# A planner of the issue order counts five times the queue time for a SyncE DMA that writes a single partition

## Chip, cores and metric

The kernel runs on one core of one Trainium2 chip. The metric is device time in microseconds (us) of one execution; the time before is the median of 3 runs, 1483.42 us (1481.35 to 1484.54).

## What is computed

One layer of a hybrid block on x of shape (1, 2048, 1024), all float32. Two branches read the same normalised input, and their gated outputs meet in one projection:

```
hn   = rmsnorm(h, mix_norm_g)
proj = hn @ w_in        # u_ssm 512 | gate_ssm 512 | q 512 | k 512 | v 512 | gate_attn 512
# SSM: 32 groups of 16 channels, 64 complex states per group, a linear recurrence over 2048 steps
y = Re(C x) + D u
zz = gelu(y) @ w_glu + b_glu
y_ssm = val * sigmoid(gate) * silu(gate_ssm)          # val, gate = halves of zz
# stick-breaking attention: 8 heads of 64, strictly causal, blocks of 128 queries
z = (rmsnorm(q) @ rmsnorm(k).T) * 64 ** -0.5
w = exp(log_sigmoid(z) + sum of log_sigmoid(-z) over the later keys)   # keys before the query only
y_att = (w @ v) * silu(gate_attn)
h = h + concat(y_ssm, y_att) @ w_out
h = h + sigmoid(rmsnorm(h, ple_norm_g) @ w_ple_gate) * (p @ w_ple_proj)
```

The attention weights of one query are a cumulative product over the keys. The kernel uses this: with s(j) the running product of sigmoid(-z), the sum of w * v becomes a sum of s times the differences of neighbouring rows of v.

## The kernel before

**Precision and tiles.** Every matmul runs as three products of float32r pieces (hi*hi, hi*lo, lo*hi), so each operand is split into two tiles, mostly by `split` (L511: a copy on ScalarE, a subtraction on VectorE). `wst` is the stage for a weight tile as it comes from HBM (L486); `w_w` is the pair that ScalarE (L491, L513) and VectorE (L65, L76) make of it.

**Stages.** The start (`phase_u`, to about 116 us) normalises x and computes u. Then the SSM is worked in batches, beside the gate matmuls `ps_sg` and the first projections of the attention (116 to 336 us). A skewed loop of 40 steps follows: the heads go in four pairs, pair hp is 8 steps behind pair hp-1, and each pair has 16 blocks of 128 queries. One step does an attention block for up to two pairs (`attn_block`) and the projections of a block that comes two steps later (`attn_proj`). From step 26 the weights `w_glu` are loaded (`glu_load`, eight tiles of 256 KB), from step 30 the GLU units run (`glu_z`, `glu_unit`), and then come products of weights that the last stage needs. The last stage (1152 us on) multiplies by w_out and w_ple_gate and writes the output.

**One block of attention.** `attn_proj` loads `xt` (L717, 1 MB, from `hn`), multiplies (`ps_q`, L745), copies half of the result to `part` (L751) and adds the halves to `qn` (L65 on VectorE). Then the differences of v: L753 copies 127 rows of v from `qn` to the v tile, shifted by one partition, and L755 copies the last row, alone, to partition 0 of the next block's v tile. GpSimd subtracts (L756), which waits for these DMAs. `rs_qk` (L507, GpSimd) and `qn` (L65) normalise q and k, TensorE turns them (`ps_tq`), ScalarE and VectorE write `q`, `k` (L788) and `g` (L791). `attn_block` computes `ps_z` (L812), ScalarE takes the sigmoid to `px` (L816), GpSimd masks the diagonal part of the block (L819, only its first chunk), VectorE scans (L821), TensorE turns (`ps_wt`, L526), ScalarE copies to `ws` (L835), TensorE multiplies by v (`ps_o`, L843), and `yat` goes to HBM by L847. `ps_tq` and `ps_wt` share one pair of PSUM banks, so a turned `ps_wt` waits until `g` has been read out of the `ps_tq` before it.

**DMA queues.** Nearly all DMAs are issued by SyncE, which the profile calls SP, in one order. An instruction that waits on SP holds back all behind it.

**What sets the order.** The program is written out once, and then `arrange` (L1556) orders each engine anew. `plan` (L1322) gives each instruction its predecessors and a modelled length from `duration` (L1289): a time on its engine, a delay until others see it, and for a DMA its bytes. `list_schedule` (L1448) takes in turn, on the engine that is free first, the ready instruction of the lowest rank; a DMA occupies its issuing engine for its modelled time only, and its data are there after a shared link of 290 KB a us and fixed delays. `best_order` (L1523) does this six times forwards and backwards; the ranks of a turn are the modelled finishing times of the one before. Of the six orders it keeps the one with the smallest modelled end, and `arrange` writes it down as a chain of dependencies on each engine. So one number in `duration` reaches every engine's order, and the instructions themselves stay the same.

Of the kernel before, what the change touches and what calls it, by code (L numbers as in the profile page):

```python
# [1288 lines left out]
def duration(i, name, outs, ins, psum):  # L1289

    n = max([a[1] for a in outs + ins] or [1])
    eng = str(i.engine).split(".")[-1]
    if name == "InstDMACopy":
        return (0.6 if eng == "Pool" else 0.45), 0.0
    if name == "InstMatmult":
        cols, kind = outs[0][1], ins[0][2]
        if i.is_transpose:
            return (0.031 if ins[0][0] <= 64 else 0.109), 0.11
        if "float32r" in kind or "bfloat16" in kind:
            return max(cols / 2400.0 + 0.0136, 0.107) / (2 if ins[0][0] <= 64 else 1), 0.11  # L1300
        half = min(outs[0][0], ins[0][0]) <= 64
        return (0.5 if outs[0][0] <= 32 else 1 if half else 2) * max(cols / 1160.0, 0.056), 0.12
    if eng == "Activation":
        return (0.05 if psum else 0.094) + n * 0.00083, 0.065 if psum else 0.03
    if eng == "Pool":
        if name == "InstTensorTensor" and "pow" in str(i.op).lower():
            return 0.35 + 0.15 * n, 0.08
        base, slope = {"InstMemset": (0.04, 0.0008), "InstTensorCopy": (0.4, 0.001), "InstTensorScalarPtr": (0.25, 0.001), "InstTensorScalarAffineSelect": (0.14, 0.0008)}.get(name, (0.12, 0.00186))
        return base + slope * n, 0.09
    if name == "InstTensorScalarPtr" and i.is_tensor_tensor_scan:  # L1310
        return 0.05 + n * 0.0022, 0.03
    if name in ("InstMemset", "InstTensorCopy", "InstTensorScalarPtr") and not psum and not i_tt(i):
        return 0.07 + n * 0.0006, 0.03
    return 0.07 + n * 0.00104, 0.03


def i_tt(i):

    return getattr(i, "is_scalar_tensor_tensor", False)


def plan(tc, pools):  # L1322
# [28 lines left out]
    for k, i in enumerate(mybir_i):  # L1351
# [65 lines left out]
        pre.append(need)  # L1417
        soft.append(loose - need)
        length.append(duration(i, type(i).__name__, outs, ins, psum) + ((outs[0][0] * outs[0][1] * 4 if type(i).__name__ == "InstDMACopy" else 0), shares(i, type(i).__name__, read, psum)))
        if type(i).__name__ == "InstMatmult":  # L1420
            mode[k] = "rows" if ins[0][0] <= 64 else "cols" if outs[0][0] <= 64 else "all"
# [194 lines left out]
```

## Time and profile before

| | |
|---|---|
| median of 3 runs | 1483.42 us |
| the profiled execution: own time | 1483.66 us |
| its span in the profile | 1481.9 us, at a granted TensorE clock of 0.995 |
| busy share of the span | TensorE (PE) 97%, its weight loads (PEld) 83%, VectorE (DVE) 68%, ScalarE (ACT) 55%, GpSimd (POOL) 32% |
| DMA packets | 178,909, 238.21 MB |

The profile is of one execution. Its own time is 1.76 us more than its span. A row of the timeline gives the start in us, the time from the start of the first to the end of the last instruction of a group, the engine, line, operation and tiles with the count, and in brackets how long the engine was idle before and what ended that idle time. Matmuls are pipelined: one may start before its predecessor's end.

### The profile page before, as it was taken

The page shows a single profiled execution, that of the slowest core. Times are in us where ns is not written, and L with a number is a line of the kernel's source. Part 1 is how long each engine was busy: PE and PEld are TensorE (multiplying, and loading weights), DVE is VectorE, ACT ScalarE, POOL GpSimd, SP SyncE. Part 2 cuts the span into 40 slices and gives each one's busy share as a digit, 9 for nine tenths or more (in the row PEclk, how much of TensorE's full clock was granted, in tenths as well). Part 3 has the DMA queues.
Part 4 walks back from the last instruction along what each step waited for, and adds up shares of the span by engine and source line. Part 5 has one row for each costly group of instructions (what it writes and reads, how often), then busy time and mean ns, then how long its engine had stood idle before and what let it go on. Part 6 is the DMA issues. An engine that isn't in the chain of part 4 may idle for free.

```text
span 1481.9 us, 33584 instructions
## 1 busy us (share of the span) xinstructions
PE 1443.8 (97%) x13068; PEld 1223.0 (83%) x13068; DVE 1011.5 (68%) x1814; ACT 810.8 (55%) x1764; POOL 473.7 (32%) x512
## 2 busy tenths in 40 slices
PE   6999999999999999999999999999999999999998
PEld 5999989988888888887788877887777888777776
DVE  8953877976567876677667775656787557844444
ACT  5654555655556765566555664566655445533332
POOL 3121364422221212121112123544234554433432
PEclk9999999999999999999999999999999999999999
DMA  8886846644433433334333455867477546423221
GB/s 292 283 284 209 246 140 195 198 158 148 142 134 107 154 119 106 117 112 144 113 109 120 130 149 175 235 224 203 118 243 246 184 152 214 140 70 100 87 73 55
DMA packets 178909, 238.21 MB, mean 161 GB/s; under 512 B 65744, under 2 KB 121024, under 8 KB 167616
## 3 DMA queue, kind: packets, MB, share of 16 engines
q1 hardware_dynamic: 176368, 227.49, 47.6%
q0 software_dynamic: 2384, 8.59, 2.0%
q8 instruction: 103, 1.69, 0.5%
q14 instruction: 54, 0.44, 0.1%
HBM read 166.94 MB, written 64.90 MB: 156 GB/s over the span
## 4 chain that ended last, share of the span: by engine, by line
PE 79%; DVE 9%; ACT 3%; issue 3%; DMA 3%; POOL 2%; SPq 0%; POOLq 0%; ACTq 0%; DVEq 0%
PE ps_q L745 21%; PE ps_o L843 7%; PE ps_z L812 6%; PE ps_wt L526 4%; PE ps_g L707 4%; PE ps_h L709 4%; PE ps_h L708 4%; PE ps_h L707 4%; PE ps_g L709 3%; PE ps_g L708 3%; PE ps_u L541 1%; PE ps_u L543 1%; PE ps_u L542 1%; POOL sx L912 1%; PE ps_sg L541 1%
## 5 line engine op out<-in xcount | busy, mean ns | idle before, releaser
L821 DVE TENSOR_TENSOR_SCAN px<-px,ps_z 128x512 f32<-128x512 f32 (+3 forms) x320 | 339.4, 1085 | 101.8 <-ACT px L816 66.1
L745 PE MATMUL ps_q<-w_w,xt 64*128 64x512 f32 x2784 | 375.9, 399 | 0.7 <-ACT part L751 0.5
L745 PEld LDWEIGHTS ps_q<-w_w,xt 64*128 64x128 f32 x2784 | 271.0, 186 | 39.0 <-DVE qn L65 1.3
L835 ACT ACTIVATE ws<-ps_wt 128x512 f32<-128x512 f32 (+3 forms) x320 | 161.1, 538 | 76.9 <-PE ps_wt L526 70.7
L816 ACT ACTIVATE px<-ps_z 128x512 f32<-128x512 f32 (+3 forms) x320 | 159.6, 535 | 75.8 <-PE ps_z L812 73.8
L812 PE MATMUL ps_z<-k,q 64*128 64x512 f32 (+3 forms) x960 | 138.9, 380 | 3.3 <-DVE px L821 2.3
L843 PE MATMUL ps_o<-ws,v 128*64 128x128 f32 x2176 | 135.9, 277 | 0.0
L843 PEld LDWEIGHTS ps_o<-ws,v 128*64 128x64 f32 x2176 | 117.8, 137 | 18.2 <-issue 15.5
L507 POOL TENSOR_TENSOR rs_qk<-rs_qk,mhalf 128x4 f32<-128x4 f32 x64 | 68.0, 1062 | 166.6 <-DVE rs_qk L72 163.8
L526 PEld LDWEIGHTS ps_wt<-ident,px 64*128 64x128 f32 x2176 | 96.0, 138 | 26.0 <-ACT ws L835 6.2
L526 PE MATMUL ps_wt<-ident,px 64*128 64x64 f32 x2176 | 102.2, 224 | 3.1 <-ACT ws L835 2.7
L812 PEld LDWEIGHTS ps_z<-k,q 64*128 64x128 f32 x960 | 88.2, 186 | 20.3 <-issue 4.9
L819 POOL TENSOR_SCALAR_AFFINE_SELECT px<-px 128x128 f32<-128x128 f32 x128 | 40.6, 327 | 170.9 <-ACT px L816 169.7
L756 POOL TENSOR_TENSOR v<-qn,v 128x128 f32<-128x128 f32 x64 | 31.4, 491 | 174.1 <-DMA v<-qn 160.4
L541 PE MATMUL ps_u<-xt,w_w 128*128 128x256 f32 x256 | 75.5, 296 | 8.1 <-ACT w_w L491 6.9
L65 DVE TENSOR_TENSOR yr<-sx,yr 128x512 fp32r<-128x512 f32 x64 | 50.6, 813 | 42.2 <-ACT yr L513 41.5
L543 PE MATMUL ps_u<-xt,w_w 128*128 128x256 f32 x256 | 74.1, 295 | 2.0 <-DVE w_w L76 2.0
L542 PE MATMUL ps_u<-xt,w_w 128*128 128x256 f32 x256 | 74.9, 294 | 0.5 <-DVE xt L65 0.5
L1026 POOL TENSOR_TENSOR sg<-sg,h 128x512 f32<-128x512 f32 x28 | 39.6, 1414 | 95.6 <-DVE sg L65 94.1
L513 ACT ACTIVATE yr<-sx 128x512 fp32r<-128x512 f32 x64 | 39.1, 627 | 55.9 <-POOL sx L912 26.2
L65 DVE TENSOR_TENSOR qn<-ps_q,part 128x512 f32<-128x512 f32 x54 | 36.8, 681 | 38.5 <-ACT part L751 35.4
L513 ACT ACTIVATE yr<-yq 128x512 fp32r<-128x512 f32 x48 | 30.3, 631 | 55.5 <-PE ps_h L709 24.2
(438 smaller groups left out, 3488.0 us busy)
## 6 DMA issues: line engine op xcount, KB each, us to landing
xt<-hn SPq DMA_DIRECT2D x58, 1024.0 KB
hn<-xt SPq DMA_DIRECT2D x16, 1024.0 KB
h<-h SPq DMA_DIRECT2D x64, 256.0 KB
wst<-in_w_in_dram SPq DMA_DIRECT2D x48, 256.0 KB
xg<-hn SPq DMA_DIRECT2D x12, 1024.0 KB
out_dram<-sg SPq DMA_DIRECT2D x32, 256.0 KB
x<-in_x_dram SPq DMA_DIRECT2D x14, 512.0 KB
h<-in_x_dram SPq DMA_DIRECT2D x28, 256.0 KB
```

The costliest lines, as they stand in the source:

```text
L526: e.nc.tensor.transpose(ps[h][:, 64 * k:64 * k + 64], v[r], e.ident[r, r])
L541: mm(out, wh, xh, start=first, stop=False)
L542: mm(out, wh, xl, start=False, stop=False)
L707: mm(out, xh, wh, start=first, stop=False, skip_group_check=more)
L708: mm(out, xh, wl, start=False, stop=False, skip_group_check=more)
L709: mm(out, xl, wh, start=False, stop=last, skip_group_check=more)
L745: nc.tensor.matmul(o, xt[r, a, c], A.w[c][r, b], start=c + s == 0, stop=c == NC8 - 1 and s == 2)
L812: nc.tensor.matmul(z[:, :n], q[half[h], a], A.k[ch][half[h], b, :n], start=s == 0, stop=s == 2)
L816: nc.scalar.activation(px[:, :n], z[:, :n], AF.Sigmoid, scale=-(HD ** -0.5))
L821: nc.vector.tensor_tensor_scan(rv, rv, z[:, :n][:, ::-1], initial=1.0 if carry[h] is None else carry[h], op0=ALU.mult, op1=ALU.bypass)
L835: nc.scalar.activation(dst, ps, AF.Copy, bias=1.0, scale=-1.0)
L843: nc.tensor.matmul(po[half[h], :P], A.v[sb][:, h], w[:, h, b], start=sb == i, stop=sb == 0)
```

## The change

```diff
@@ -1291,6 +1291,8 @@ def duration
     n = max([a[1] for a in outs + ins] or [1])
     eng = str(i.engine).split(".")[-1]
     if name == "InstDMACopy":
+        if eng != "Pool" and outs and outs[0][0] == 1:
+            return 2.2, 0.0
         return (0.6 if eng == "Pool" else 0.45), 0.0
     if name == "InstMatmult":
```

`outs[0][0]` is the number of partitions written. The new case holds for 64 DMAs, all on SP: the 60 copies of a last row at L755 and four copies of one row at L727 (from `vl`, a spare tile, to the v tile). They are the same DMAs as before; only the planner counts 2.2 us of SP's time for each, in place of 0.45 us. Lines behind L1293 have moved by two. No instruction is added or removed.

The order changes in stretches and stays in others. By the times of the profile before it differs at 16 to 35 us, 91 to 106, 116 to 336, 475 to 526, 683 to 755, 816 to 1152 and in one place near 1258; it is the same, up to single neighbours, at 345 to 475, 526 to 683, 755 to 816 and in the rest of the last stage. Three places follow.

**SP, 686 to 705 us: the first loads of `w_glu`.** Two of the eight tiles have been issued at 674 us; the rows below begin with the next ones. Rows with a minus are those of before, rows with a plus those of the change.

```order
-L486 DMA wst<-in_ssm_w_glu_dram 128x1x512 x3
+L486 DMA wst<-in_ssm_w_glu_dram 128x1x512 x2
 L717 DMA xt<-hn_69 128x2048
 L753 DMA v<-qn 127x128
 L755 DMA v<-qn 1x16x8
 L847 DMA ya_103<-yat 128x128
-L486 DMA wst<-in_ssm_w_glu_dram 128x1x512
+L486 DMA wst<-in_ssm_w_glu_dram 128x1x512 x2
 L717 DMA xt<-hn_61 128x2048
```

The fifth tile of `w_glu` has moved behind one block's `xt`, both copies of v, and the store of another block's result.

**ACT at the same place, 689 to 697 us.** `w_w<-wst` at L513 is the first half of the split of such a tile. Before:

```order
L788 ACTIVATE k<-ps_tq,gq 128x128
L513 ACTIVATE w_w<-wst 128x512
L791 ACTIVATE g<-ps_tq 128x128
L816 ACTIVATE px<-ps_z 128x512 x2
L751 ACTIVATE part<-ps_q 128x512
L513 ACTIVATE q<-ps_tq 128x128
L513 ACTIVATE w_w<-wst 128x512
L788 ACTIVATE k<-ps_tq,gq 128x128
```

With the change:

```order
L788 ACTIVATE k<-ps_tq,gq 128x128
L816 ACTIVATE px<-ps_z 128x512
L791 ACTIVATE g<-ps_tq 128x128
L816 ACTIVATE px<-ps_z 128x512
L751 ACTIVATE part<-ps_q 128x512
L513 ACTIVATE q<-ps_tq 128x128
L513 ACTIVATE w_w<-wst 128x512 x2
L788 ACTIVATE k<-ps_tq,gq 128x128
```

The third tile's split stood between one block's `k` and `g`. Now it stands with the fourth tile's behind the next block's `q`, ahead of that block's `k` and `g`.

**DVE, 703 to 709 us**, in the same stretch: `qn` of L76 is the one from which the next two v copies on SP read; the two `px` rows are the scans of a block's diagonal chunk, which come behind GpSimd's L819.

```order
 L65 TENSOR_TENSOR qn<-qn,rs_qk 128x256
+L821 SCALAR_TENSOR_TENSOR px<-px,ps_z 128x384 x2
 L76 SCALAR_TENSOR_TENSOR qn<-ps_q,rs_148,part 128x512
-L821 SCALAR_TENSOR_TENSOR px<-px,ps_z 128x384 x2
-L764 TENSOR_REDUCE ssq<-sq 128x4
```

`qn` has moved behind the two scans.

**ACT, 851 to 857 us: where the GLU stage starts.** `zr<-zt` is the first half of a split of the GLU's input, `ws` is what TensorE's next turning waits for. Before:

```order
L759 ACTIVATE gn<-qn 128x128
L513 ACTIVATE zr<-zt 128x512 x2
L835 ACTIVATE ws<-ps_wt 128x2x2x64
L513 ACTIVATE zr<-zt 128x512
L835 ACTIVATE ws<-ps_wt 128x2x2x64
L816 ACTIVATE px<-ps_z 128x256 x2
```

With the change:

```order
L835 ACTIVATE ws<-ps_wt 128x2x2x64 x2
L816 ACTIVATE px<-ps_z 128x512 x2
L762 ACTIVATE sq<-qn 128x256
L759 ACTIVATE gn<-qn 128x128
L513 ACTIVATE zr<-zt 128x512
L835 ACTIVATE ws<-ps_wt 128x8x64
L513 ACTIVATE zr<-zt 128x512
L835 ACTIVATE ws<-ps_wt 128x8x64
```

Both `ws` of 128x2x2x64 now stand ahead of all pieces of `zr`, and the pieces alternate with the `ws` of the next chunk.

## The prediction

> **What bounds the kernel now.** I read the page first, for the engine that sets the end, then the busy time by stretches, for the idle time that a new order could win, and then the timelines of the places where the order changes.
>
> ```profile
> PE 1443.8 (97%) x13068; PEld 1223.0 (83%) x13068; DVE 1011.5 (68%) x1814; ACT 810.8 (55%) x1764; POOL 473.7 (32%) x512
> PE 79%; DVE 9%; ACT 3%; issue 3%; DMA 3%; POOL 2%; SPq 0%; POOLq 0%; ACTq 0%; DVEq 0%
> ```
>
> TensorE is busy for 1443.8 of 1481.9 us, and the chain that ended last lies on it for 79%. SP's own issues take 0% of the chain. No instruction is added or removed, so TensorE's work stays as it is, and all that an order can win is its idle time: 1481.9 - 1443.8 = 38.1 us, spread over the program. The next view gives the stretches with the new order: the window, its length, then the busy time of PE, PEld, DVE, ACT and POOL.
>
> ```profile
> 116.00:336.00 220.00, 214.19 (x1779) 201.43 (x1778) 169.73 (x298) 118.49 (x275) 83.79 (x60) 1.00 0.61 191
> 683.00:722.00 39.00, 34.80 (x410) 27.52 (x408) 26.33 (x42) 23.01 (x54) 6.62 (x12) 0.97 0.39 111
> 850.00:866.00 16.00, 15.06 (x194) 11.94 (x192) 14.85 (x23) 13.44 (x28) 4.26 (x6) 1.00 0.59 138
> 905.00:1107.00 202.00, 200.08 (x1905) 160.47 (x1902) 140.09 (x183) 122.46 (x244) 86.86 (x88) 1.00 0.66 203
> ```
>
> TensorE is idle for 5.8 us in the first, 4.2 in the second, 0.9 in the third and 1.9 in the last. The second is the densest in idle time, 39 us that hold 4.2; there the new order matters most.
>
> **The charge itself: nothing.** The 64 DMAs remain, so their real time on SP stays.
>
> ```profile
> L755 SPq DMA_DIRECT2D v<-qn x56: 567/2338/6853, 195.9 to 1017.0; - x56
> L727 SPq DMA_DIRECT2D v<-vl x4: 503/544/552, 311.0 to 783.4; - x4
> ```
>
> The columns are least, median and greatest ns. At L755 a median of 2.338 us fits the new 2.2 us. The four of L727 write one partition too and take 0.544 us, so the time is not that of a single partition. The timeline of SP shows whose it is:
>
> ```profile
> 433.39 0.67 SPq L753 DMA_DIRECT2D v<-qn  x1
> 434.14 2.34 SPq L847 DMA_DIRECT2D ya<-yat  x1
> 436.55 0.99 SPq L755 DMA_DIRECT2D v<-qn  x1
> ```
>
> Here a store of 128 partitions came between the two copies of v and paid 2.34 us, and L755 got by with 0.99. So the charge falls on whatever stands directly behind L753, which copies 127 rows. Nearly always that is L755, before and after, so the planner's SP becomes right in sum though the reason is wrong, and I price the charge at 0: SP has no share of the chain, and its slack covers the places where a store takes L755's place. If that cover were gone, one such swap would cost 2.34 - 0.99 = 1.35 us of SP once.
>
> [...]
>
> **683 to 722 us, first stall.** SP, then ACT, then PE:
>
> ```profile
> 686.35 7.89 SPq L486 DMA_DIRECT2D wst<-in_ssm_w_glu_dram  x3
> 694.30 0.47 SPq L717 DMA_DIRECT2D xt<-hn  x1
> 695.74 0.68 SPq L753 DMA_DIRECT2D v<-qn  x1
> 696.47 6.39 SPq L755 DMA_DIRECT2D v<-qn  x1
> ...
> 703.66 0.61 SPq L486 DMA_DIRECT2D wst<-in_ssm_w_glu_dram  x1
> 704.33 0.46 SPq L717 DMA_DIRECT2D xt<-hn  x1
> 705.59 0.64 SPq L753 DMA_DIRECT2D v<-qn  x1
> ```
>
> ```profile
> 692.34 0.63 ACT L513 ACTIVATE w_w<-wst 128x512 fp32r<-128x512 f32 x1 [2.90 <-DMA wst<-in_ssm_w_glu_dram]
> ...
> 694.92 0.63 ACT L513 ACTIVATE w_w<-wst 128x512 fp32r<-128x512 f32 x1 [0.16 <-DMA wst<-in_ssm_w_glu_dram]
> 695.46 0.35 ACT L788 ACTIVATE k<-ps_tq,gq 128x128 fp32r<-128x128 f32 x1
> 695.80 0.42 ACT L762 ACTIVATE sq<-qn 128x256 f32<-128x256 f32 x1
> 696.23 0.28 ACT L791 ACTIVATE g<-ps_tq 128x128 f32<-128x128 f32 x1
> ```
>
> ```profile
> 689.68 1.55 PE L745 MATMUL ps_q<-w_w,xt 64*128 64x512 f32 x12
> 693.18 0.34 PE L526 MATMUL ps_tq<-ident,qn 64*128 64x64 f32 x4 [1.96 <-ACT g L791]
> ```
>
> ACT waits 2.90 us for the third tile of w_glu with `g` behind it, and PE stands idle for 1.96 us because `ps_tq` needs `g`. In the new order `g`, two `px` and `part` pass ahead of that split, so this stall goes. What is late next: both splits now stand ahead of the next block's `k` and `g`, and the fourth tile lands only at 694.92. Before, `k`, `sq` and `g` came behind that split and `g` ended at 696.23 + 0.28 = 696.51; now it is `k`, one `px` and `g`, about 0.1 longer. TensorE's next `ps_wt` needs that `g`, so it starts at 696.6, as before, whatever TensorE does sooner ahead of it. The stall moves by 3 us of program and comes back: **+0.1 us**, between -1.96 (TensorE gets work to cover it) and +1 (the fourth tile slips).
>
> **The two stalls behind it.** GpSimd waits for the v copies, and all of it behind L756 waits too, the masks of L819 among them, on which DVE's scans and then PE's next `ps_z` wait:
>
> ```profile
> 706.22 0.46 POOL L756 TENSOR_TENSOR v<-qn,v 128x128 f32<-128x128 f32 x1 [4.26 <-DMA v<-qn]
> ...
> 716.27 0.45 POOL L756 TENSOR_TENSOR v<-qn,v 128x128 f32<-128x128 f32 x1 [5.84 <-DMA v<-qn]
> ```
>
> ```profile
> 707.39 0.39 PE L812 MATMUL ps_z<-k,q 64*128 64x512 f32 x1
> 707.97 0.96 PE L812 MATMUL ps_z<-k,q 64*128 64x512 f32 x5 [0.18 <-DVE px L821]
> ...
> 716.18 0.39 PE L812 MATMUL ps_z<-k,q 64*128 64x512 f32 x1
> 718.28 0.97 PE L812 MATMUL ps_z<-k,q 64*128 64x512 f32 x5 [1.70 <-DVE px L821]
> ```
>
> Five of these matmuls span 0.96 us and one 0.39, so one follows another after (0.96 - 0.39) / 4 = 0.14 us. The stalls cost 707.97 - 707.39 - 0.14 = 0.44 and 718.28 - 716.18 - 0.14 = 1.96 us.
>
> The first v copy was issued at 695.74 and landed at 706.2, behind 256 KB of w_glu and 1 MB of `xt`. With the change `xt` has not the fifth tile ahead of it and can go when `ps_q` has released its buffer, at 689.68 + 1.55 = 691.2, some 3 us earlier; `part` and `qn` come about 2 us earlier as well. The copy should land by 702, and GpSimd is no longer late: **-0.44 us** (0 to -0.44). The second copy was issued at 705.59 and landed at 716.3, again behind a w_glu tile and an `xt`. The sixth tile can now go once its buffer is free, near 701, since L755 no longer blocks SP until 702.9; that wins up to 2 us for the `xt` behind it. Against this, `qn` now stands behind two scans:
>
> ```profile
> 704.77 0.75 DVE L76 SCALAR_TENSOR_TENSOR qn<-ps_q,rs,part 128x512 f32<-128x512 f32 x1 [0.99 <-ACT part L748]
> 706.96 1.80 DVE L821 TENSOR_TENSOR_SCAN px<-px,ps_z 128x384 f32<-128x384 f32 x2 [1.44 <-POOL px L819]
> ```
>
> If the scans start near 704.5, `qn` ends near 704.5 + 1.8 + 0.75 = 707.05, against 705.5, and the copy is issued 1.5 us later, while its queue is free 2 us earlier. Half of the stall is my middle: **-1.0 us** (0 to -1.96).
>
> **850 to 866 us.**
>
> ```profile
> 851.58 2.21 ACT L513 ACTIVATE zr<-zt 128x512 fp32r<-128x512 f32 x2
> 853.67 0.39 ACT L835 ACTIVATE ws<-ps_wt 128x256 f32<-128x256 f32 x1
> 853.93 1.20 ACT L513 ACTIVATE zr<-zt 128x512 fp32r<-128x512 f32 x1
> 854.97 0.44 ACT L835 ACTIVATE ws<-ps_wt 128x256 f32<-128x256 f32 x1
> ```
>
> ```profile
> 853.12 1.55 PE L745 MATMUL ps_q<-w_w,xt 64*128 64x512 f32 x12
> 855.46 0.71 PE L526 MATMUL ps_wt<-ident,px 64*128 64x64 f32 x16 [0.79 <-ACT ws L835]
> ```
>
> Three pieces of `zr`, 3.4 us, stood ahead of or between the two `ws`, and PE was idle for 0.79 us. Both `ws` now stand ahead of them: **-0.8 us**. The pieces go between later `ws`, one of 1.20 us ahead of each, so the stall may come back there: 0 is the other end.
>
> **The other stretches.** At the start, 16 to 35 us, TensorE waits for a chain over GpSimd, ACT and DVE that has the same members in a slightly different order; I take 0. In 116 to 336 and 905 to 1107 us the reshuffle is wide, and I cannot follow each wait by hand. TensorE's idle time there, 5.8 and 1.9 us, bounds the gain at 7.7; a loss of as much is my estimate of the other end. I take 0 as the middle.
>
> **The sum**: 0 + 0.1 - 0.44 - 1.0 - 0.8 = -2.1 us. Against the profiled execution's 1483.66 this gives 1481.6; that execution is 0.24 us above the median of the runs, 1483.42. I predict **1481.6 us**.
>
> **Rivals.**
> *Stalls only change place (1483.5 us).* For it: the stall at 693 already comes back at 696.6 by the sum above, and TensorE at 97% leaves a new order little. The wrong address of the charge belongs here, too: the planner gets SP's sum right by accident, and SP decides nothing. Against it: the wait for v at 706 and 716 hangs on two queue entries that really move.
> *Slower, the chain v, GpSimd, scan, qn, next v (1488 us).* In the new order of DVE the `qn` from which the second copy reads stands behind two scans, which wait for L819, which waits behind L756 for the first copy. If that copy still lands at 706, the scans end at 706.96 + 1.80 = 708.8, `qn` at 709.5, and the second copy starts at 709.6 in place of 705.59: 4.0 us later, and the stall of 1.96 becomes 6. That is 1483.66 + 4.0 = 1487.7. It decides from a landing of the first copy later than about 704. For it: the copy is issued behind 1 MB of `xt` in the same queue, and L755 took 6.39 us there. Against it: the fifth tile, which delayed `xt`, is out of its way.
> *Faster, the wide stretches win too (1477 us).* If half of their 7.7 us of idle time goes as well, 1481.6 - 3.9 = 1477.7. Nothing in the rows says that it does; the idle time only allows it.
>
> **How the numbers follow.** I give the forecast 0.40, the stalls in new places 0.25, the slower chain, or a new wait of its size in the wide stretches, 0.22, and the wide gain 0.13. The range reaches from 1474 (1483.66, less the 7.7 us of the wide stretches and the 2.1 of the sum) to 1490 (1483.66, plus 4.0 for the chain and 2.4, the size of the two v stalls, once more elsewhere). A measurement of this kernel can tell about 0.2%, 3.0 us, from no change, which puts the bounds at 1480.5 and 1486.4. The forecast lies 1.1 us inside the lower one: of its 0.40 I put 0.17 below, 0.19 within and 0.04 above. With the other cases: faster 0.30 (0.17 + 0.13), same 0.40 (0.19 + 0.21 of the second), slower 0.30 (0.04 + 0.04 + 0.22).
>
> **What would show it.** Right: PE's idle time between 683 and 722 us falls from 4.2 to about 3, the row of L756 near 706 has no wait for the DMA worth 4 us, the first `ps_wt` behind 695 us is released by `g`, and the `ps_wt` near 855 has no wait for `ws`. L755's median stays near 2.3 us and L727's near 0.54. Wrong: `qn` of L76 later than 708 with a longer idle time behind it (the slower chain), or PE's idle time in 116 to 336 or 905 to 1107 us off by more than 2 us, where my sum has 0.

## The result and the profile after

The change made the kernel slower: 1498.69 us (median of 4 runs, 1495.13 to 1500.25) against 1482.68 us before on the same chips (1481.35 to 1484.54), a ratio of 1.0104 with a 95% interval of 1.0092 to 1.0116. The prediction was 1481.6 us, with a range of 1474 to 1490. The page of the profile after, its first part and its chain:

```profile
span 1498.4 us, 33594 instructions
...
PE 1452.3 (97%) x13068; PEld 1228.0 (82%) x13068; DVE 1014.4 (68%) x1814; ACT 812.1 (54%) x1764; POOL 467.5 (31%) x512
...
PE 77%; DVE 8%; DMA 5%; ACT 4%; issue 3%; POOL 3%; SPq 0%; POOLq 0%; DVEq 0%; ACTq 0%
```

The span has grown by 16.5 us, and it falls into two parts. TensorE's idle time went from 38.1 to 46.1 us, +8.0. Its busy time went from 1443.8 to 1452.3 us, +8.5, although it ran the same 13068 records: the same work took longer. To see where, the program is cut at places where both orders stand alike, so that each stretch holds the same matmuls. The columns are the window, its length, PE's busy time with its records, the granted clock, and the DMA share and GB/s. Before:

```profile
0.00:106.10 106.10, 90.63 (x800) 0.95 0.84 295
106.10:364.40 258.30, 252.49 (x2204) 1.00 0.59 186
673.60:756.90 83.30, 79.10 (x1002) 0.98 0.38 117
807.10:1143.90 336.80, 333.95 (x3202) 1.00 0.64 191
```

After:

```profile
0.00:108.60 108.60, 92.48 (x801) 0.94 0.82 287
108.60:379.50 270.90, 258.68 (x2204) 0.97 0.56 178
689.20:770.40 81.20, 78.31 (x1004) 0.98 0.36 117
820.50:1160.00 339.50, 334.71 (x3202) 1.00 0.62 189
```

| stretch | change in us | of it idle | predicted |
|---|---|---|---|
| start | +2.5 | +0.7 | 0 |
| SSM batches to the first attention blocks | +12.6 | +6.4 | 0, bounded at 7.7 with the GLU's |
| first w_glu loads | -2.1 | -1.3 | -1.3 |
| GLU stage | +2.7 | +1.9 | -0.8 |

The place that the prediction worked out improved, and the stretch that it took at 0 lost 12.6 us. There the granted clock is 0.97 on the mean, and finer windows, the first two from the end of the start, show why:

```profile
70.20:73.60 3.40, 2.10 (x26) 1.00 0.96 340
73.60:77.10 3.50, 3.50 (x19) 0.51 1.03 376
189.70:193.10 3.40, 1.12 (x7) 1.00 0.25 92
193.10:196.50 3.40, 3.40 (x10) 0.50 0.24 84
322.80:326.20 3.40, 1.11 (x11) 1.00 0.32 116
326.20:329.60 3.40, 3.08 (x14) 0.51 0.63 201
343.30:346.70 3.40, 2.10 (x33) 1.00 0.93 322
346.70:353.50 6.80, 6.03 (x42) 0.50 0.59 226
281.90:285.30 3.40, 2.14 (x19) 1.00 0.01 2
285.30:288.70 3.40, 2.45 (x22) 1.00 0.52 189
```

In four of these pairs a window of 3.4 us in which TensorE was idle for 1.3 to 2.3 us is followed by one or two such windows at half the clock, and each of these, where TensorE works throughout, costs another 1.7 us, half of 3.4 by its clock of 0.50 or 0.51. In the last pair the idle time lies on both sides of a border, 1.3 and 0.9 us, and the clock stays. In matmuls of one kind, step by step behind the stall that ends at 192.41 us:

```profile
192.41 0.47 PE L707 MATMUL ps_qk<-w_w,xg 128*128 128x512 f32 x1 [2.27 <-DVE gsq L65]
192.72 0.39 PE L708 MATMUL ps_qk<-w_w,xg 128*128 128x512 f32 x1
192.95 0.47 PE L709 MATMUL ps_qk<-w_w,xg 128*128 128x512 f32 x1
193.22 0.63 PE L707 MATMUL ps_qk<-w_w,xg 128*128 128x512 f32 x1
193.64 0.63 PE L708 MATMUL ps_qk<-w_w,xg 128*128 128x512 f32 x1
```

The step from one to the next is 0.23 us from 192.72 to 192.95 and 0.42 from 193.22 to 193.64. Both executions have 10.2 us at half the clock near 30 us. Behind that and ahead of the end, before had one such window, the 3.4 us from 719.5, right after the stall at 716 of the prediction:

```profile
716.10:719.50 3.40, 1.70 (x14) 1.00 0.00 0
719.50:722.90 3.40, 3.40 (x27) 0.51 0.39 104
```

After has five stretches of six windows in all (73.6, 193.1, 326.2, 346.7 and 711.9 us; the rows of the last stand with the run warm below). Half of TensorE's busy time in them is (3.50 + 3.40 + 3.08 + 6.03 + 3.00) / 2 = 9.5 us, against 3.40 / 2 = 1.7 us before: 7.8 of the 8.5 us by which the busy time grew.

The three longest stalls of the long stretch, 2.27, 2.21 and 1.68 of its 12.2 us of idle time, are of one kind: TensorE's next instruction needs a PSUM bank that the GELU's chain (`gsq`, ACT and DVE in turn) still reads. The one of 0.93 us ahead of the third waits likewise for a gate's product (`sg`).

```profile
286.25 0.46 PE L461 MATMUL ps_y<-us,tp 128*128 128x128 f32 x2 [2.21 <-DVE gsq L65]
...
324.29 0.55 PE L812 MATMUL ps_z<-k,q 64*128 64x128 f32 x6 [0.93 <-DVE sg L65]
326.52 2.07 PE L745 MATMUL ps_q<-w_w,xg 64*128 64x512 f32 x8 [1.68 <-DVE gsq L65]
```

Before had one stall of this kind there:

```profile
316.35 0.97 PE L745 MATMUL ps_q<-w_w,xg 64*128 64x512 f32 x6 [1.57 <-DVE gsq L65]
```

### The profile page after: what moved, and what is told of

Same layout as the page of the kernel before. It is cut to its first block, busy times and chain, and to the rows that moved or that the text cites. A ratio compares the mean times of both kernels' runs of the same rounds, so it can differ in the third digit from the quotient of the medians.

```text
span 1498.4 us, 33594 instructions
## 1 busy us (share of the span) xinstructions
PE 1452.3 (97%) x13068; PEld 1228.0 (82%) x13068; DVE 1014.4 (68%) x1814; ACT 812.1 (54%) x1764; POOL 467.5 (31%) x512
## 4 chain that ended last, share of the span: by engine, by line
PE 77%; DVE 8%; DMA 5%; ACT 4%; issue 3%; POOL 3%; SPq 0%; POOLq 0%; DVEq 0%; ACTq 0%
PE ps_q L745 21%; PE ps_o L843 7%; PE ps_z L812 6%; PE ps_wt L526 4%; PE ps_g L707 3%; PE ps_h L707 3%; PE ps_h L709 3%; PE ps_h L708 3%; PE ps_g L709 3%; PE ps_g L708 3%; PE ps_u L543 1%; PE ps_u L542 1%; PE ps_u L541 1%; POOL sx L912 1%; DVE rot L65 1%
## 5 line engine op out<-in xcount | busy, mean ns | idle before, releaser
L819 POOL TENSOR_SCALAR_AFFINE_SELECT px<-px 128x128 f32<-128x128 f32 x128 | 41.5, 334 | 175.0 <-ACT px L816 167.1
L513 ACT ACTIVATE yr<-sx 128x512 fp32r<-128x512 f32 x64 | 39.2, 628 | 56.4 <-POOL sx L912 26.1
L513 ACT ACTIVATE yr<-yq 128x512 fp32r<-128x512 f32 x48 | 30.3, 631 | 56.4 <-PE ps_h L709 28.6
```

## The experiments

All times are medians; every ratio is to the kernel before, on the same chip, with its 95% interval. The planner's "own count" in the expectations is the modelled end of an order, replayed with the costs of before: 1411.8 us for the order of before and 1419.9 us for the change's. Replayed with the new charge, the order of before still ends at 1416 to 1417. So by the very costs that the change gave it, the planner found a worse order than the one it had; these are its own numbers, not times. The search has not settled when it stops: from the fifth to the sixth forward pass its order of before went from 1414.0 to 1411.8, and with the charge it went from 1419.9, which was kept, to 1422.9. The diffs below show the deciding lines only, some in short form, with the name of the run as a comment; the code around them is left out.

**Where: one half of each order.** `new` is the change's order, `old` that of before; they are joined where both hold the same instructions on every engine.

```diff
+    order = splice(old, start, new, (400,), True)    # early_new; late_new: False
```

> The order of the change up to about 415 us of the program, the order of before behind it. Theory 'early': the loss sits in the wide stretch ahead of 400 us, where the change's first matmuls behind 400 us came 15.2 us later than before's; then 1483 + 15 = 1498 us (1495 to 1500). Rival 'everywhere': every reordered stretch loses in proportion to its length; the early ones hold about half of the reordered time, then 1490 us (1488 to 1493).

> The order of before up to about 415 us, the order of the change behind it. Theory 'early': 16.5 us of delay at the end less 15.2 us at 400 us leave 1.4, so 1484.5 us (1482 to 1487). Rival 'everywhere': half of the loss, 1490 us (1488 to 1493).

Measured: early_new 1494.74 us, 1.0076 (1.0061 to 1.0091); late_new 1487.14 us, 1.0019 (1.0006 to 1.0031). Of the change's 1.04%, 0.76% go with the order of the first 415 us and 0.19% with the rest. Both times lie just outside the ranges of 'early' (0.3 us below and 0.1 above) and 5 and 3 us off the 1490 of 'everywhere'.

**Why: the charge, or the search.**

```diff
+    for k in single[:1]:      # first1; rest63: single[1:]; l753: the 64 copies of 127 rows
+        length[k] = (2.2,) + tuple(length[k][1:])
```

> The planner counts 2.2 us for the first of the 64 single-partition copies alone (the copy of v's last row near 196 us); the other 63 cost 0.45 us as before. Theory 'search': what the charge says of the queue does not matter; any small nudge near 200 us throws the six turns of the search onto another order, and the time goes with that order: 1490 to 1500 us. Rival 'charge': the loss comes from what the 64 charges do to SP's order, each its share; one of 64 gives 1483.5 us (1482 to 1485).

> The planner counts 2.2 us for all of the 64 single-partition copies but the first. Theory 'search': another order again, no worse than by chance; nearly all of the charge is there, yet the time may lie anywhere between 1480 and 1500 us, and I expect it nearer to before, 1486 us (1482 to 1491), as the order ahead of 200 us stays that of before. Rival 'charge': 63 of 64 shares of the loss, 1498 us (1495 to 1501).

> The planner counts 2.2 us for the 64 copies of 127 partitions (L753), behind which the slow issue stands, and 0.45 us again for the single-partition ones. Theory 'wrong address': the change lost because the charge stood on the wrong DMA; with the right one the order is as good as before or better: 1484 us or less (1478 to 1486). Theory 'search': it is one more nudge, and the order gets worse as the planner's own count of it, replayed with the old costs, gets worse. That count goes with the five times measured so far at about 1.8 us for each us; this order's is 5.2 us above that of before, so 1493 us (1489 to 1497).

Measured: first1 1496.18 us, 1.0085 (1.0070 to 1.0100); rest63 1486.84 us, 1.0027 (1.0015 to 1.0039); l753 1491.86 us, 1.0055 (1.0040 to 1.0070). One charge out of 64, 1.75 us on one instruction near 196 us, costs 12.3 us alone (1496.18 - 1483.84), where all 64 cost 16; the other 63 without it cost 3.0. The loss is not a sum over the DMAs. The profile of first1 has a granted clock of 0.96 from 39.6 to 81.8 us and of 0.98 from 117.7 to 348, where the change's has 0.95 from 39 to 82.5 and 0.98 from 118.5 to 351.2; on TensorE the one charge leads to the change's own order up to about 460 us of the planner's time. So first1 says which charge brought the early order; it is not a second, independent order. Nor does the charge on the DMA of 127 rows help, behind which the slow issue stands; there the time that the theory 'search' worked out from the planner's count came true (1489 to 1497).

Three more kernels nudge the search without saying anything of these DMAs, or say it only once.

```diff
-        return (0.6 if eng == "Pool" else 0.45), 0.0
+        return (0.6 if eng == "Pool" else 0.4411561), 0.0     # sp044
-def best_order(ops, pre, soft, length, mode, rows, turns=6):
+def best_order(ops, pre, soft, length, mode, rows, turns=9):  # turns9
+        # last_only: the charged lengths in the sixth forward pass alone
```

> No charge on a single-partition DMA; the cost of every DMA on SP goes from 0.45 to 0.4411561 us, a change of 2% that says nothing of the queue. Theory 'search': any such nudge lands on another order, and this one's own count, replayed with the old costs, is 2.3 us below that of before; at 1.8 us for each us this gives 1480 us (1476 to 1483.5), faster than both kernels. Rival 'chance': the planner's count says nothing at this distance, and a new order is as a rule worse: 1484 to 1492 us.

> No cost is changed; the search makes nine turns instead of six and keeps the order that its own count likes best, 0.5 us below the one of before. Some 2500 of 11720 matmuls stand elsewhere. Theory 'chance': among orders that the planner counts as equal the chip differs by several us, and a new one is rather worse, as the 2% nudge of all of SP's DMAs was (1488.8): 1487 us (1483 to 1493). Rival 'the planner's count decides': 1483 us (1481.5 to 1484.5).

> All 64 single-partition copies are counted at 2.2 us, but only in the sixth and last forward pass of the search; the five before it and all backward passes count 0.45 us, and the sixth order is kept. Theory 'search': one pass with the new count moves few instructions (some 500 of 11720 matmuls stand elsewhere than before, against some 4400 with the change); the loss needs the ranks to drift over six turns, so 1485.5 us (1482 to 1489). Rival 'charge': the charge itself pushes SP's neighbours to bad places, in one pass as well as in six: 1495 to 1499 us.

Measured: sp044 1488.82 us, 1.0031 (1.0019 to 1.0043); turns9 1484.82 us, 1.0008 (0.9999 to 1.0018); last_only 1486.00 us, 1.0019 (1.0009 to 1.0028). A change of 2% that means nothing costs 5 us, although the planner counts its order as the better one: here my reading of the planner's count failed, and its count is no guide below a few us. turns9 fits 'chance' and misses the other range by 0.3 us. The full charge in the last pass alone costs 2.7 us; the 16 us came only with the charge in every pass. How many passes it takes was not tested.

**What a stall is worth, and whether filling one place helps.**

```diff
+    order = splice(old, start, new, (640, 845), False)                            # place12
+    move(line, gsq_step, sg); move(line, gsq_last, rot); move(line, gsq_sigmoid, swp)  # gsq_back
+            nc.tensor.matmul(pq[0], xt[:, 0, 0], A.w[0][:, 0], start=True, stop=True)  # warm, ten times
```

> The order of before, but from about 665 to 880 us that of the change: the two places on which the prediction's gains rest. Theory 'local gains are real': where the change's own run went through 685 to 755 us, its delay fell from 15.6 to 13.4 us, and by 860 us to 12.3; so about 2 to 3 us faster than before, 1481 us (1479 to 1483). Rival 'stalls only change place': the same as before, 1483.8 us (1482.5 to 1485.5), as the planner's own count says, which differs by 0.1 us.

> The change's order with three instructions put back where before had them: near 188 us, on VectorE the two steps of one gsq chain ahead of the sg and of the rot product, on ScalarE its sigmoid ahead of the two half copies of swp. Theory 'stall and clock': the stall of 2.3 us at 190 us was this chain's, and the 3.4 us at a granted clock of 0.5 behind it were the stall's; both go, 2.3 + 1.7 = 4 us, so 1494.7 us (1493 to 1497) and no low clock near 193 us. Rival 'idle only': the stall goes and the clock falls all the same, 1496.4 us. Rival 'moves on': the next instruction waits in its place, 1498.7 us as the change.

> The change's order, with ten matmuls more that have no use (128x512, into a PSUM bank that the next group overwrites), placed ahead of the six matmuls before TensorE's stall of 2.6 us at 709.6 to 712.4. Theory 'idle brings the low clock': with the stall filled, the 3.4 us at a granted clock of 0.5 that followed it do not come; from 705 to 725 us the kernel gains up to 1.7 us on the change's own course, 1497.5 us (1494 to 1500). Rival 'the low clock has another cause': it comes all the same near 712, and the ten matmuls cost up to 1 us.

Measured: place12 1482.83 us, 0.9994 (0.9986 to 1.0003). Within the interval that is no change, and the value lies in the ranges of both theories. In its trace the local gains are there, and a new stall gives part back:

```profile
697.17 0.59 PE L526 MATMUL ps_wt<-ident,px 64*128 64x64 f32 x12 [2.44 <-ACT g L791]
```

This is the wait for `g` that the prediction saw move from 693 to 697 us, now with 3.4 us at half the clock behind it.

gsq_back: 1503.08 us, 1.0121 (1.0106 to 1.0136), not faster than the change, and above all three expectations. In its trace the stall at 190 us is gone, and by 194 us it had gained 4.1 us, as the first theory had it. Then the next projection waits instead, and the clock falls there:

```profile
198.37 0.50 PE L707 MATMUL ps_qk<-w_w,xg 128*128 128x512 f32 x1 [2.83 <-ACT qn L735]
```

```profile
195.80:199.20 3.40, 0.83 (x4) 1.00 0.03 10
199.20:202.60 3.40, 3.40 (x10) 0.51 0.17 54
```

The third theory, that the stall moves on, fits the trace: to put this one wait right wins nothing. That holds for this wait; the others were not tried.

warm: 1497.33 us, 1.0100 (1.0084 to 1.0115). The change's own windows around its stall at 709.6 to 712.4, and those of warm:

```profile
708.50:711.90 3.40, 1.47 (x10) 1.00 0.80 252
711.90:715.40 3.50, 3.00 (x24) 0.51 0.21 57
```

```profile
708.00:712.00 4.00, 4.00 (x51) 1.00 0.29 90
712.00:716.00 4.00, 4.00 (x56) 1.00 0.25 81
```

With ten useless matmuls in the stall the half clock does not come, and warm gains 1.6 us on the change's course: it is 706.53 - 704.06 = 2.47 us ahead at the `ps_o` in front of the stall and 715.60 - 711.54 = 4.06 at the second `ps_wt` behind it. In one profiled execution each, but with the sign and size expected, idle time brought the low clock, at a cost of up to 1.7 us for each 3.4. The time of the whole program does not show it (1.0100 against 1.0104 for the change, with overlapping intervals): at the end of the two profiles warm is 1498.4 - 1495.2 = 3.2 us ahead, so 0.9 of the 4.06 was lost again behind this place.

**What the charge speaks of.** Is SP's time worth anything, and whose are the 2.3 us?

```diff
+        nc.sync.dma_start(A.v[i + 1][:1]..., vr[P - 1:])                     # twice755, behind L755, unseen by the planner
+        nc.sync.dma_start(e.two_d[16 * A.hp + i:16 * A.hp + i + 1], vr[P - 1:])   # twice_free, likewise
-    nc.sync.dma_start(vb[1:], vr[:P - 1])                                     # split753
+    nc.sync.dma_start(vb[1:113], vr[:112])
+    nc.sync.dma_start(vb[113:], vr[112:P - 1])
```

> The order of before, with a second, identical copy of the last row of v behind each of the 60 copies at L755 (the planner does not see it; 60 DMAs more on SP, of 0.5 to 2.3 us each). Theory 'SP is free': SP has no share in the chain, so the time of these DMAs costs next to nothing, 1484.5 us (1482.5 to 1487). Rival 'SP's time counts': if what the charge speaks of were worth charging, 60 such copies would cost a good part of 60 x 0.57 = 34 us, 1495 us or more.

> The order of before, with a second DMA of the same last row behind each of the 60 copies at L755, into 60 rows of a scratch tensor in HBM that nothing else uses, so that it waits for nothing; the planner does not see it. The run with a second copy into the same place does not settle what SP's time is worth, since each second copy there waited 3 to 4 us for the first to land and held SP. Theory 'SP is free': 60 more issues cost next to nothing, 1484.5 us (1482 to 1487). Rival 'SP's time counts': at 0.5 to 2.3 us each the copies hold up the next xt and v, and a good part of 30 to 130 us appears, 1495 us or more.

> The order of before, with the copy of 127 rows of v (L753) cut in two, 112 rows and 15 rows, one directly behind the other; the planner sees one copy of 127 rows. [...] Rival 'the single partition is the slow one': L755 stays at 2.3 us, one more DMA a block makes it 1484 us or more.

Measured: twice755 1539.54 us, 1.0369 (1.0326 to 1.0412), far from what I expected. Its timeline shows what the extra copy did:

```profile
460.74 3.91 SPq L755 DMA_DIRECT2D v<-qn  x1
468.07 0.50 SPq L757 DMA_DIRECT2D v<-qn  x1
```

It writes where the first one writes, so the program lets it be issued only when that one has landed, 468.07 - 464.65 = 3.4 us later, and all of SP waits. This run prices a wait on SP of that size, at 56 / 60 = 0.9 us a block; it says nothing of SP's issue time. twice_free, with a free destination, does: 1485.00 us, 1.0008 (0.9999 to 1.0017). Its 60 extra issues last 0.42 us at the median and cost no more than 0.17%. Issues of 2.3 us or more were not added in any run.

split753: 1480.01 us, 0.9973 (0.9962 to 0.9984): **faster than both kernels**, and closer together, 1478.4 to 1480.5. The copies of its v rows, 112, 15 and then the single one (L758 here):

```profile
L753 SPq DMA_DIRECT2D v<-qn x64: 517/534/3906, 194.7 to 1036.4; - x64
...
L755 SPq DMA_DIRECT2D v<-qn x64: 818/852/927, 195.3 to 1037.0; - x64
...
L758 SPq DMA_DIRECT2D v<-qn x56: 526/546/1779, 196.3 to 1013.5; - x56
...
POOL v L759 <- DMA v<-qn: 76.0, 45, 9.0
```

GpSimd's wait before:

```profile
POOL v L756 <- DMA v<-qn: 160.4, 59, 7.6
```

The single-partition copy takes 0.546 us at the median, where it took 2.338, so the single partition is not the slow one. GpSimd's wait for v falls from 160.4 to 76.0 us in total. The program gains at one place, the one where the prediction looked for it. There GpSimd waits 2.09 us for the second v copy, where it waited 5.84, and the same matmuls as in the row of before at 673.60 take less time:

```profile
710.87 0.46 POOL L759 TENSOR_TENSOR v<-qn,v 128x128 f32<-128x128 f32 x1 [2.09 <-DMA v<-qn]
...
673.50:752.50 79.00, 76.79 (x1002) 1.00 0.40 123
```

The same 1002 matmuls took 83.3 us before and take 79.0, with no window at half the clock. At this place two things change at once: the v copies land earlier, and SP is no longer held for the 6.39 us that L755 took there. The run does not part them.

## Why the prediction was wrong

**The charge itself, 0: right.** L755's median after is 2.302 us and L727's 0.544, as before:

```profile
L755 SPq DMA_DIRECT2D v<-qn x56: 922/2302/5891, 201.3 to 1033.4; - x56
...
L727 SPq DMA_DIRECT2D v<-vl x4: 502/544/552, 320.7 to 797.0; - x4
```

The DMAs themselves stayed as they were. split753 shows that the slow issue comes from the copy of 127 rows ahead of it: the charge stood on its neighbour. What the prediction called SP's slack is shown by twice_free for issues of 0.42 us; the 3.4 us waits of twice755 were not covered, and whether the 6.39 us at L755 are is open.

**First stall, moved and returned: right in kind.** The `ps_wt` behind it waits for `g`, as said; its idle time is 2.44 us in place of 1.96, and the half clock came with it, which the sum did not have.

```profile
712.40 0.90 PE L526 MATMUL ps_wt<-ident,px 64*128 64x64 f32 x12 [2.44 <-ACT g L791]
```

**The two stalls of v, -1.4: right, and too small.** Both are gone, and with the second the half clock at 719.5. The stretch gained 2.1 us net. The rows are those of the two `ps_z` that waited before:

```profile
725.46 0.97 PE L812 MATMUL ps_z<-k,q 64*128 64x512 f32 x6
...
732.91 0.94 PE L812 MATMUL ps_z<-k,q 64*128 64x512 f32 x6
```

**850 to 866 us, -0.8: right at the place, lost behind it.** The two `ws` waits that followed a piece of `zr` came back as idle times of 0.33 and 0.23 us, and a wait of 1.19 us appeared at 881.9. The bound of 0 was nearer than the sum's -0.8.

```profile
868.02 0.71 PE L526 MATMUL ps_wt<-ident,px 64*128 64x64 f32 x16 [0.33 <-ACT ws L835]
...
871.11 0.71 PE L526 MATMUL ps_wt<-ident,px 64*128 64x64 f32 x16 [0.23 <-ACT ws L835]
...
881.89 0.34 PE L526 MATMUL ps_tq<-ident,qn 64*128 64x64 f32 x4 [1.19 <-ACT ws L835]
```

**The other stretches, 0, with a loss of at most 7.7: wrong, and this step sank the prediction.** The loss was 2.5 us at the start and 12.6 in the stretch to 364 us, and the GLU stage, where the sum had -0.8 at one place and 0 for the rest, lost 2.7. Two things failed in it. I took a wide reshuffle of a good order as likely to gain as to lose; first1, rest63, l753, sp044 and last_only all lost, by 2.7 to 12.3 us, and turns9 came out even within its interval. That is a handful of orders, of which first1 shares the change's early part. And I priced stalls by their idle time. Here 6.4 us of idle time brought 6.2 us more of slowed matmuls, so my bound was well below the loss. The prediction's own sign of being wrong, idle time in 116 to 336 us off by more than 2 us, is met by the 6.4. Before's own row at 683 to 722 us, with a granted clock of 0.97, had this in it and I read past it.

**The rival "slower, the chain v, GpSimd, scan, qn, next v"** gave the right sign for a reason that did not occur: its stretch gained. Its chance of 0.22 also named a new wait of its size in the wide stretches; that came, but as several waits and a slower clock, three times the 4 us priced.

What stays open is why just this first charge leads the search so far off, and what a fair sample of orders would cost. That the gate matmuls, which wait for nothing, are spent too early in the new order is only argued from the traces: with one wait repaired, gsq_back met the next.

## What to carry to other kernels

In a planner that searches by feedback, a small change of cost need not be a small change of order: one cost of one instruction can send it to another one. So replay old and new order under the same costs, and measure, before a cost is called better. When such a change moves most of the program, expect a loss, not 0, as the middle of the places you cannot follow (so it was in these few orders), and price a stall of about 2 us on TensorE at nearly twice its idle time (an estimate from the 6.4 us of idle time here, which came with 6.2 us of slowed matmuls). If a DMA is slow, mend the DMA rather than tell the planner: cutting 127 rows into 112 and 15 won what no charge did (1480.01 us).

## What the runs showed of the hardware

**The clock fell after partly idle windows.** In the change's record of the granted clock the single half clocks last 3.413 us, and their starts lie whole multiples of that apart, 119.46 = 35 x 3.413 between 73.66 and 193.12 us. In the profiles of before and of the change, from 45 us on and ahead of the last instructions, a stretch at half the clock begins six times. In the 3.4 us directly ahead TensorE was idle for 1.70 us before, and for 1.30, 2.28, 2.29, 1.30 and 1.93 us with the change (3.40 less the busy time in the windows above). Cut into windows from these starts, neither profile has another window there with 1.70 us or more of idle time; below that it went either way: behind 313.3 to 316.8 us of before, with 3.50 - 1.93 = 1.57 us of idle time, and behind 1278.6 to 1282.0 us of the change, with 3.40 - 1.74 = 1.66, the clock stayed at 1.00. The stall of 2.21 us at 286.25 us escaped: it was split over two windows, with 1.3 and 0.9 us of idle time (the last two rows of the windows shown above). The half clock near 30 us begins at 30.04 us in the profile of before and at 29.28 in that of the change, whose order differs from 16 us on. Whether such starts shift from run to run, and whether that is behind the wider spread of the slower kernels (late_new 1481.6 to 1491.1 us), no run shows.

**Here the DMA behind a copy of 127 rows was slow to issue.** The copy of a single row takes 2.338 us at the median behind 127 rows and 0.546 behind 112 and 15; a store of 128 partitions behind the 127 rows took 2.34 (the row at 434.14 us in the prediction). Why it is the next DMA that waits, no run shows.
